# A two-layer mixed-attention MoE block on one core: small token blocks of an expert in one go, and the loop for left-over tokens in the midst of the experts

## Chip, cores, metric

One core of a Trainium2 chip runs the whole program; nothing is shared with other cores. The metric is the device time in microseconds, of the kernel before the median of three runs.

## What is computed

Two layers over 512 image tokens and, in the first layer, 256 context tokens, width 1024: three kinds of attention, a merge of their outputs, then a mixture of 16 experts of which each token takes two. The change touches the experts alone:

```python
def moe_ffn(tokens, w_router, b_router, w_gate, w_up, w_down):
    ...
    def expert_block(args):
        xb, e = args
        hid = jax.nn.silu(xb @ w_gate[e]) * (xb @ w_up[e])
        return hid @ w_down[e]

    y = lax.map(expert_block, (buf.reshape(n_blocks, MOE_BLOCK, d), block_e)).reshape(-1, d)
    contrib = y[dest] * sw[:, None].astype(y.dtype)
    return jnp.zeros_like(tokens).at[st].add(contrib)
```

`w_gate` and `w_up` are 1024 x 512 for each expert, `w_down` 512 x 1024, all float32. The result of a token is the weighted sum of its two experts.

## The kernel before

**Places for tokens.** The program is fixed ahead of the routing, so each of 16 places ("slots") takes one expert and a set number of tokens: `LINES` (line 1885) gives a letter for each. B is a `Block` of 128 tokens, S a `Half` of 64, P both together, 128+64, for the most wanted experts. Layer 0 has `BBBBPBSBBPBSBPBS`: three P, at slots 4, 9 and 13. Layer 1 has `BBBSBSSBSSBSSBSS`, no P. Slots 0 to 2 hold fixed experts; the router sorts the others by how many tokens they got. A token record lies in a table in DRAM; POOL fetches records (`lrec`), gathers their rows (`xg`) and, at an expert's end (`finish`, `add_up`, line 1567), adds the weighted output into DRAM (`yd` in layer 0, `xa` in layer 1).

**Left-over tokens.** Tokens that find no place are served by `late_block` (line 1705), a whole expert on 128 of them, in a loop whose trip count `nmore` the router works out (line 2095). The loop, `tc.For_i` in lines 1771 and 1772, stands ahead of all experts of a layer: behind the first gathers (`next_fetch`), ahead of SP's 13 reads of the expert order (line 1776) and of the first transposes. `LB` is the number of weight buffer sets in its body.

**Weights.** `Weights` (line 38) streams all weights in 512 KB chunks in a fixed list, four for each of gate (G), up (U) and down (D) of an expert. `load` issues the next chunk's DMA on SP whenever a raw buffer is free; in layer 0's experts there are 24 raw buffers, in layer 1's 31. `make` splits a chunk for a Block into two parts (`wh` on ScalarE, `wl` on VectorE, lines 102 and 114), after which its raw buffer goes back; there is room for the parts of four chunks. A Half reads the raw chunk itself. At a P slot the chunk is kept raw as well (`keep`) until `free`.

**TensorE.** A Block takes six matmuls a chunk, in three terms (`mm3`), stationary 128 columns, moving 512. A Half takes matmuls on two column halves of 64 (`up` in line 1654, `down` in 1679). Both are recorded under line 174, so the names tell them apart: `g<-wh,xH` or `yps<-wh,hidT` is a Block's, `g<-raw,xs` or `ysm<-raw,hidS` a Half's. For each slot the order is: transposes of the next slot's tokens (`turn`), up product of this slot, half of the next slot's gate product, transposes of this slot's hidden values (`hidden`), the other half, this slot's down product, `finish`. The helper that the change replaces takes the blocks of a slot chunk by chunk:

```python
ch = ws.get()
for i, b in enumerate(blocks[s]):
    b.up(ps[i], *words(b, ch), c)
used(ch)
```

Of the kernel before, what the change touches and what calls it, by code (L numbers as in the profile page):

```python
# [23 lines left out]
PG1 = 14  # L24
MW = 8
EX = {0: 3, 1: 5}
LB = 2
RING = 10


# [7 lines left out]
class Weights:  # L38
# [95 lines left out]
    def free_raw(self, c):  # L134
        self.live[id(c.raw_pool)] -= 1
        c.raw_pool = None
        self.load()

    def free(self, c):

        if c.part_pool is not None:
            self.live[id(c.part_pool)] -= 2
        if c.part_pool is None or c.keep:
            self.free_raw(c)
# [3 lines left out]
def tile_dit(ctx, tc, a, out):  # L148
    nc = tc.nc
# [8 lines left out]
    def acc_tile(name="acc"):  # L158
        return psum.tile([128, 512], F32, tag="acc", name=name)
# [21 lines left out]
    def split(h, l, src):  # L181
        nc.scalar.copy(h, src)
        nc.vector.tensor_tensor(l, src, h.bitcast(F32), op=OP.subtract)
# [59 lines left out]
    def w_of(l, what, e, c):  # L243

        w = a[{"G": "w_gate", "U": "w_up", "D": "w_down"}[what]][l]
        return w[e, c] if isinstance(e, int) else w[bass.ds(e, 1), c].rearrange("o p n -> (o p) n")
# [81 lines left out]
    ws = Weights(nc, specs)  # L328
# [144 lines left out]
    def mod_row(pool, tag, l, j, v, name):  # L473
        t = pool.tile([128, D], F32, tag=tag, name=name)
        nc.sync.dma_start(t, bc(modd[l][j, v, :], D))
        return t
# [1061 lines left out]
    def moe(l, R, late, ex):  # L1538
# [15 lines left out]
        def yo_tile():  # L1554
            return mx.tile([128, D], F32, tag="yo", name="yo", bufs=YO[l])

# [141 lines left out]
        def words(b, ch):  # L1698
            return (ch.raw,) if isinstance(b, Half) else (ch.h, ch.l)

        def used(ch):
            ws.pump(2, LEAD)
            ws.free(ch)

        def late_block(j):

            r = mx.tile([128, 4], I32, tag="rec2", name="rec2", bufs=1)
            at = mx.tile([128, 1], I32, tag="at2", name="at2", bufs=1)
            lst = mx.tile([128, 2, SLOTS], I32, tag="lst", name="lst", bufs=1)
            R.rest(lst, yo_tile())  # L1710
            nc.vector.tensor_copy(at, lst[:, 1, bass.ds(j, 1)])
            R.record(r, at)
            e = nc.values_load(lst[0:1, 0, bass.ds(j, 1)], engines=[mybir.EngineType.SP], min_val=0, max_val=NE - 1)
            w = [[mw.tile([128, 1024], dt, tag="mw", name=f"w2{i}{n}") for n, dt in enumerate((F32, F32R, F32R))]
                 for i in range(LB)]

            def part(what, i):
                raw, h, lo = w[i % LB]
                nc.sync.dma_start(raw, w_of(l, what, e, i % 4))
                split(h, lo, raw)  # L1720
                return h, lo

            b = Block(r)
            b.fetch(yo_tile())
            b.turn()
            g, u = acc_tile("g2"), acc_tile("u2")
            for i in range(8):
                b.up(g if i < 4 else u, *part("GU"[i // 4], i), i % 4)
            b.silu(g)
            b.times(u)  # L1730
            b.hidden()
            b.sums()
            for k in range(4):
                b.down(*part("D", 8 + k), k)
            b.finish()


        blocks, records = [], {}
        for s in range(NE):
# [4 lines left out]
            bs = [Half(lrec[:, s, :], slot=s) if kind == "S" else Block(lrec[:, s, :])]  # L1744
            records[bs[0]] = lrec[:, s, :], place(l, s)
            if kind == "P":
                i = PLACED[l].index(s)
# [6 lines left out]
        def next_fetch():  # L1754
            if queue:
                queue.pop(0).fetch()

        def next_record():
            if later:
                out_, i = records[later.pop(0)]  # L1760
                R.record(out_, R.pat[:, i:i + 1])

        def ahead():
            next_fetch()
            next_record()
# [2 lines left out]
        ws.low()  # L1768
        for _ in range(XG[l]):
            next_fetch()  # L1770
        with tc.For_i(0, nc.values_load(R.nmore[0:1, 0:1], min_val=0, max_val=SLOTS)) as j:
            late_block(j)
        ws.limit = first_in + NEAR if l == 0 else len(ws.specs)
        ws.load()
        for s in range(AHEAD, NE):
# [5 lines left out]
        ahead()  # L1781
        next_record()

        def gate(s, c0, c1, ps, done=None):

            for c in range(c0, c1):
                ch = ws.get()
                for i, b in enumerate(blocks[s]):
                    b.up(ps[i], *words(b, ch), c)
                    if c == 3 and done:  # L1790
                        done(i)
                used(ch)

        def products(s, name):
            return [b.product(name) for b in blocks[s]]

        def silus(s, ps):
            for b, p in zip(blocks[s], ps):
                b.silu(p)

        gp = products(0, "g")
        gate(0, 0, 4, gp)
        silus(0, gp)
        for s in range(NE):
            nx = s + 1 < NE
            if nx:
                for b in blocks[s + 1]:
                    b.turn()
                    ahead()
            up = products(s, "u")  # L1810
            gate(s, 0, 4, up, lambda i: blocks[s][i].times(up[i]))
            if nx:
                gp = products(s + 1, "g")
                gate(s + 1, 0, HIDAT, gp)
            for b in blocks[s]:
                b.hidden()
            if nx:
                gate(s + 1, HIDAT, 4, gp)
                silus(s + 1, gp)
            for b in blocks[s]:  # L1820
                b.sums()
            for k in range(4):
                ch = ws.get()
                for b in blocks[s]:
                    b.down(*words(b, ch), k)
                used(ch)
            if l == 0 and not nx:
                ws.pump(4 * len(TURN) + WEND)
            ws.low()
            for b in blocks[s]:  # L1830
                b.finish()
            if l == 0 and s == NE - 2:
                for j in range(2):
                    gt2.append(mod_row(pool0, "pg", 0, j, 5, f"gt2{j}"))
# [7 lines left out]
    for l in range(2):  # L1842
        ws.set_pools(2 * l, *mixer_pools)
        mixer(l)
        moe(l, *merge(l))
# [30 lines left out]
HT = {0: 2, 1: 1}  # L1876
TROWS = 896
MORE = 6
YO = {0: 2, 1: 1}
XG = {0: 2, 1: 1}  # L1880
NS = NE - AHEAD
SLOTS = 14
# [11 lines left out]
LEAD = 3  # L1894
# [23 lines left out]
class Router:  # L1918
# [3 lines left out]
    def __init__(self, tc, nc, rt, small, l, nt, tri, ones, br, oac_tile, tabd):  # L1922
# [10 lines left out]
        self.cap = small([128, NE], F32, "cap")  # L1933
        self.more = small([128, MORE, NE], F32, "more")
        self.spacer = small([1, 1], F32, "spacer")
        self.scat = []

    def prepare(self):
# [20 lines left out]
        nc.vector.memset(self.cap, 128.0)  # L1959
        nc.gpsimd.iota(self.more, pattern=[[128, MORE], [0, NE]], base=0, channel_multiplier=0,  # L1960
                       allow_small_or_imprecise_dtypes=True)
# [108 lines left out]
    def arrange(self, count):  # L2070
# [21 lines left out]
        tt(over, count, self.cap, op=OP.subtract)  # L2092
        tt(self.more, over[:, None, :].to_broadcast([128, MORE, NE]), self.more, op=OP.is_gt)
        nc.vector.reduce_sum(flag, self.more.rearrange("p b e -> p (b e)"), axis=AX.X)
# [142 lines left out]
```

## Time and profile before

| | |
|---|---|
| median of three runs | 2968.36 us (2964.67 to 2971.39) |
| profiled execution | 2971.79 us, span 2970.0 us |
| TensorE busy | 2774.9 us (93%), granted clock 0.969 in the mean |
| VectorE, ScalarE, GpSimd busy | 1835.0, 1279.9, 355.3 us |
| DMA | 557.63 MB, mean 188 GB/s |
| experts of layer 0, of layer 1 | about 1345 to 1663, and 2683 to 2946 us |

Times of the rows further down are microseconds from the start of the span. PE is TensorE, PEld its weight loads, DVE VectorE, ACT ScalarE, POOL GpSimd; SPq is SyncE's queue, which issues the weight DMAs. In brackets stands how long the engine was idle before an instruction and who released it. A busy share near 1 over the whole run says little by itself: the stages have different limits, so the stretches are read one by one.

### The profile page before, as it was taken

To read this page: it belongs to the slowest core of one execution; us is meant where nothing else is said; L and a number is where in the kernel's file an instruction comes from. 1 tells how busy PE (TensorE), PEld (TensorE's weight loads), DVE (VectorE), ACT (ScalarE), POOL (GpSimd) and SP (SyncE) were. 2 spreads that over 40 slices of the span, in tenths; PEclk is the share of its full clock that TensorE was granted. 3 is DMA by queue.
4 is the path that set the end of the run, shared out by engine and by line. 5 is a ranking of instruction groups with operands and counts; after the bars stand their busy time and mean duration, and the time that the engine had idled before them with its cause. 6 is when DMAs were issued, how large, how long until landed. Compare 5 with 4: busy or idle time off the path is not lost. (4 is left out here: it accounts for less than half of the span.)

```text
span 2970.0 us, 41952 instructions
## 1 busy us (share of the span) xinstructions
PE 2774.9 (93%) x15152; PEld 2221.7 (75%) x15152; DVE 1835.0 (62%) x3340; ACT 1279.9 (43%) x2370; POOL 355.3 (12%) x415
## 2 busy tenths in 40 slices
PE   7999999999999999979999699999999999978985
PEld 4888888888888766767666378878888887767653
DVE  4676567666554455677676566667776655677543
ACT  4444445445443211217575354444455442226332
POOL 1220000000010000022222131100000100012311
PEclk8999999999999999989999899999999999988998
DMA  6333222213243566758999732222223447589997
GB/s 240 131 110 105 89 75 91 91 65 103 100 156 118 211 240 238 273 225 304 328 370 363 256 122 82 89 78 97 75 96 123 146 153 285 207 304 341 370 367 293
DMA packets 201910, 557.63 MB, mean 188 GB/s; under 512 B 25158, under 2 KB 49862, under 8 KB 201696
## 3 DMA queue, kind: packets, MB, share of 16 engines
q1 hardware_dynamic: 173888, 503.63, 47.0%
q0 software_dynamic: 10688, 25.02, 3.5%
q10 hardware_dynamic: 17120, 26.23, 2.4%
q8 instruction: 121, 1.98, 0.3%
q14 instruction: 93, 0.76, 0.1%
HBM read 461.94 MB, written 96.77 MB: 188 GB/s over the span
## 5 line engine op out<-in xcount | busy, mean ns | idle before, releaser
L114 DVE TENSOR_TENSOR wl<-raw,wh 128x1024 fp32r<-128x1024 f32 x474 | 564.6, 1221 | 130.7 <-ACT wh L102 123.8
L102 ACT CAST wh<-raw 128x1024 fp32r<-128x1024 f32 x474 | 484.4, 1050 | 352.0 <-DMA raw<-oT 105.0
L887 ACT ACTIVATE P<-sc,st 128x768 f32<-128x768 f32 (+4 forms) x240 | 176.3, 734 | 339.9 <-DVE st L885 213.4
L885 DVE TENSOR_REDUCE st<-sc 128x1 f32<-128x768 f32 (+4 forms) x240 | 178.6, 744 | 121.5 <-PE sc L174 115.7
L174 PE MATMUL psb<-wl,wh 128*128 128x512 f32 x480 | 189.6, 395 | 8.1 <-DVE wl L114 8.0
L921 ACT CAST ptH<-pt 128x512 fp32r<-128x512 f32 x264 | 142.9, 591 | 125.0 <-PE pt L906 104.5
L174 PE MATMUL psb<-wh,wh 128*128 128x512 f32 x480 | 192.9, 402 | 1.7 <-ACT wh L102 1.7
L174 PE MATMUL psb<-wh,wl 128*128 128x512 f32 x480 | 189.1, 394 | 2.0 <-DVE wl L114 2.0
L931 DVE TENSOR_TENSOR ptL<-pt,ptH 128x512 fp32r<-128x512 f32 x264 | 169.6, 681 | 9.3 <-ACT ptH L921 9.1
L906 PE MATMUL pt<-ident,P 128*128 128x128 f32 x1056 | 141.5, 275 | 13.9 <-ACT P L887 10.9
L906 PEld LDWEIGHTS pt<-ident,P 128*128 128x128 f32 x1056 | 119.5, 141 | 45.2 <-ACT P L887 31.3
L174 PE MATMUL psR<-wh,hH 128*128 128x512 f32 (+1 forms) x384 | 150.8, 393 | 0.0
L174 PE MATMUL psR<-wl,hH 128*128 128x512 f32 (+1 forms) x384 | 147.1, 383 | 2.7 <-DVE wl L114 2.7
L174 PE MATMUL psR<-wh,hL 128*128 128x512 f32 (+1 forms) x384 | 147.6, 384 | 0.0
L893 DVE TENSOR_SCALAR P<-P,st 128x768 f32<-128x768 f32 (+3 forms) x240 | 130.0, 542 | 8.5
L174 PEld LDWEIGHTS psb<-wh,wh 128*128 128x128 f32 x480 | 91.1, 190 | 47.5 <-issue 19.3
L481 POOL TENSOR_SCALAR rstd<-ss 128x4 f32<-128x4 f32 (+2 forms) x70 | 22.0, 314 | 835.3 <-ACT h L487 303.1
L174 PEld LDWEIGHTS psb<-wl,wh 128*128 128x128 f32 x480 | 91.1, 190 | 29.1 <-DVE wl L114 11.5
L174 PE MATMUL sc<-swkT,swqs 128*128 128x256 f32 x704 | 109.1, 281 | 2.2 <-ACT P L887 2.2
L174 PEld LDWEIGHTS psb<-wh,wl 128*128 128x128 f32 x480 | 91.1, 190 | 22.9 <-DVE wl L114 3.6
L174 PE MATMUL yps<-wh,hidT 128*128 128x512 f32 x320 | 105.7, 397 | 0.0
L1094 DVE COPY sc<-sink 128x1 f32<-128x1 f32 x160 | 25.7, 161 | 128.5 <-PE sc L174 122.3
(495 smaller groups left out, 6916.4 us busy)
## 6 DMA issues: line engine op xcount, KB each, us to landing
raw<-in_w_in_dram SPq DMA_DIRECT2D x136, 512.0 KB
raw<-in_w_gate_dram SPq DMA_DIRECT2D x128, 512.0 KB
raw<-in_w_up_dram SPq DMA_DIRECT2D x128, 512.0 KB
raw<-in_w_down_dram SPq DMA_DIRECT2D x128, 512.0 KB
raw<-in_w_mod_dram SPq DMA_DIRECT2D x96, 512.0 KB
raw<-in_w_br_dram SPq DMA_DIRECT2D x48, 512.0 KB
raw<-oT SPq DMA_DIRECT2D x30, 512.0 KB
raw<-in_w_out_dram SPq DMA_DIRECT2D x16, 512.0 KB
```

The source lines that it names most:

```text
L102: self.nc.scalar.copy(c.h, c.raw)
L114: self.nc.vector.tensor_tensor(c.l, c.raw, c.h.bitcast(F32), op=OP.subtract)
L174: nc.tensor.matmul(ps, lhs, rhs, start=start, stop=stop, skip_group_check=share)
L481: nc.gpsimd.tensor_scalar(r[:, 0:cnt], ss, four / n, four * EPS, op0=OP.mult, op1=OP.add)
L885: nc.vector.reduce_max(st[:, 1, h:h + 1], s[:, 0:self.ns], axis=AX.X, negate=True)
L887: nc.scalar.activation(self.P[h][:, 0:self.ns], s[:, 0:self.ns], AF.Exp, bias=st[:, 1, h:h + 1], accum_out=st[:, 2, h:h + 1])
L893: nc.vector.tensor_scalar(self.P[h][:, 0:self.nk], self.P[h][:, 0:self.nk], st[:, 3, h:h + 1], None, op0=OP.mult)
L906: nc.tensor.transpose(pt[:, c * 256 + h * 128:c * 256 + (h + 1) * 128], self.P[2 * x + h][:, i * 128:(i + 1) * 128], ident)
L921: nc.scalar.copy(ph, src)
L931: nc.vector.tensor_tensor(pl, src, ph.bitcast(F32), op=OP.subtract)
L1094: nc.vector.tensor_copy(s[:, nk:nk + 1], sink[:, hd:hd + 1])
```

## The change

At a P slot, all four chunks of a product go through the Block first; each gives its parts back (`free_parts`) but stays raw in `kept`, and then the Half takes all four. This holds for gate, up and down (`chunk`). The loop for left-over tokens moves from ahead of the experts to behind slot 10 in layer 0 and slot 13 in layer 1 (`LOOPAT`), behind that slot's `finish`. Its body has one weight buffer set instead of two.

```diff
--- before.py
+++ after.py
@@ -24,7 +24,7 @@
 PG1 = 14
 MW = 8
 EX = {0: 3, 1: 5}
-LB = 2
+LB = 1
 RING = 10
 
 
@@ -135,6 +135,11 @@
         self.live[id(c.raw_pool)] -= 1
         c.raw_pool = None
         self.load()
+
+    def free_parts(self, c):
+
+        self.live[id(c.part_pool)] -= 2
+        c.part_pool = None
 
     def free(self, c):
 
@@ -1768,8 +1773,6 @@
         ws.low()
         for _ in range(XG[l]):
             next_fetch()
-        with tc.For_i(0, nc.values_load(R.nmore[0:1, 0:1], min_val=0, max_val=SLOTS)) as j:
-            late_block(j)
         ws.limit = first_in + NEAR if l == 0 else len(ws.specs)
         ws.load()
         for s in range(AHEAD, NE):
@@ -1781,15 +1784,33 @@
         ahead()
         next_record()
 
+        kept = []
+
+        def chunk(bs, c, step, done=None):
+
+
+            ch = ws.get()
+            step(0, c, words(bs[0], ch))
+            if c == 3 and done:
+                done(0)
+            if len(bs) == 1:
+                used(ch)
+                return
+            ws.pump(2, LEAD)
+            ws.free_parts(ch)
+            kept.append(ch)
+            if c == 3:
+                for i, ch in enumerate(kept):
+                    step(1, i, words(bs[1], ch))
+                    ws.free(ch)
+                kept.clear()
+                if done:
+                    done(1)
+
         def gate(s, c0, c1, ps, done=None):
 
             for c in range(c0, c1):
-                ch = ws.get()
-                for i, b in enumerate(blocks[s]):
-                    b.up(ps[i], *words(b, ch), c)
-                    if c == 3 and done:
-                        done(i)
-                used(ch)
+                chunk(blocks[s], c, lambda i, k, w: blocks[s][i].up(ps[i], *w, k), done)
 
         def products(s, name):
             return [b.product(name) for b in blocks[s]]
@@ -1820,15 +1841,15 @@
             for b in blocks[s]:
                 b.sums()
             for k in range(4):
-                ch = ws.get()
-                for b in blocks[s]:
-                    b.down(*words(b, ch), k)
-                used(ch)
+                chunk(blocks[s], k, lambda i, c, w: blocks[s][i].down(*w, c))
             if l == 0 and not nx:
                 ws.pump(4 * len(TURN) + WEND)
             ws.low()
             for b in blocks[s]:
                 b.finish()
+            if s == LOOPAT[l]:
+                with tc.For_i(0, nc.values_load(R.nmore[0:1, 0:1], min_val=0, max_val=SLOTS)) as j:
+                    late_block(j)
             if l == 0 and s == NE - 2:
                 for j in range(2):
                     gt2.append(mod_row(pool0, "pg", 0, j, 5, f"gt2{j}"))
@@ -1876,6 +1897,7 @@
 HT = {0: 2, 1: 1}
 TROWS = 896
 MORE = 6
+LOOPAT = {0: 10, 1: 13}
 YO = {0: 2, 1: 1}
 XG = {0: 2, 1: 1}
 NS = NE - AHEAD
```

TensorE in layer 0, slot 4, end of the first and start of the second chunk of the up product, before (`raw` are chunks as the Half reads them):

```order
L174 MATMUL u<-wl_13592,xH 128x512
L174 MATMUL u<-wh_13591,xL 128x512
L174 MATMUL u<-raw_13203,xs 64x256 x4
L174 MATMUL u<-wh_13601,xH 128x512
L174 MATMUL u<-wl_13602,xH 128x512
L174 MATMUL u<-wh_13601,xL 128x512
```

and of the change, the end of the same product:

```order
L179 MATMUL u<-wl_13431,xH 128x512
L179 MATMUL u<-wh_13430,xL 128x512
L179 MATMUL u<-raw_12989,xs 64x256 x4
L179 MATMUL u<-raw_13001,xs 64x256 x4
L179 MATMUL u<-raw_13013,xs 64x256 x4
L179 MATMUL u<-raw_13047,xs 64x256 x4
L179 MATMUL g<-wh_13440,xH 128x512
```

The Half's matmuls of four chunks stand together instead of one chunk's between two of the Block's.

SP at the end of layer 1, before: the last down weights of slot 15, then the final gain and the rows for the output.

```order
L83 DMA raw_27178<-in_w_down_dram 128x1024
L83 ISA
L83 DMA raw_27180<-in_w_down_dram 128x1024
L1852 DMA gf<-in_g_final_dram 128x1024
L1856 DMA cx_27423<-xa_116 128x1024
```

Of the change, with the semaphores that a row waits for (DMAHW are the eight that SP's DMAs raise):

```order
L83 DMA raw712_26961<-in_w_down_dram 128x1024 [waits DMAHW7_49,PE_49]
L83 ISA
L83 DMA raw713_26963<-in_w_down_dram 128x1024 [waits DMAHW0_49,DVE_49]
L1851 TENSOR_LOAD nmore_23306
L1851 ISA x2
L1851 COMPARE_AND_BRANCH
L1851 UNCONDITIONAL_BRANCH [waits SP_sequencer_49,DMAHW0_49,DMAHW1_49,DMAHW2_49,DMAHW3_49,DMAHW4_49,DMAHW5_49,DMAHW6_49,DMAHW7_49]
```

The loop of layer 1 now stands behind the same last down weights of slot 15 (`raw713` is the last chunk of the list), so behind the loads of all 20 chunks that slots 14 and 15 still use, and ahead of the final gain.

## Rows read from the trace of the kernel before

**Rows 1.** Stretches (us, busy by engine and count, PEclk, DMA share, GB/s): layers 0, 1, 1
```profile
1420.00:1445.00 25.00, 25.00 (x134) 17.07 (x134) 17.07 (x16) 15.52 (x18) 4.51 (x3) 1.00 0.92 313
...
2900.00:2925.00 25.00, 23.34 (x150) 15.72 (x148) 14.36 (x16) 9.43 (x12) 5.03 (x3) 1.00 1.03 385
...
2831.00:2834.00 3.00, 2.31 (x12) 1.79 (x14) 0.00 (x0) 0.49 (x1) 1.87 (x2) 0.66 0.98 386
```

**Rows 2.** Timeline (start, us, engine, line, instruction, idle before): start of layer 0's experts
```profile
1333.65 0.98 POOL L1549 DMA_INDIRECT xg<-h2d,rec  x1 [4.93 <-SPq L1771]
...
1341.79 1.97 PE L493 MATMUL xbt<-ident,xg 128*128 128x128 f32 x8 [17.05 <-SPq L1776]
...
1349.70 0.63 PE L174 MATMUL g<-wl,xH 128*128 128x512 f32 x1
```

**Rows 3.** Landings by line: layer 0's first gather, its middle adds, the last add
```profile
DMA to landing us min/median/max: 4.4/4.4/4.4
...
DMA to landing us min/median/max: 8.8/8.8/8.8
...
DMA to landing us min/median/max: 3.7/3.7/3.7
```

**Rows 4.** DMA issues of layer 1's experts: gathers, median us to landing
```profile
xg<-h2d,lrec POOLq DMA_INDIRECT x13, 10.0
```

**Rows 5.** Line of the loop, layer 1 (count, ns min/median/max, first and last start)
```profile
L1771 SPq COMPARE_BRANCH  x2: 33/38/44, 2672.8 to 2675.6; - x2
...
L1771 SPq EVENT_SEMAPHORE  x12: 27/28/28, 2678.4 to 2679.1; - x12
```

**Rows 6.** Timeline: start of layer 1's experts
```profile
2671.53 0.33 SPq L1563 DMA_DIRECT2D gt2row<-modd  x1
...
2680.06 1.97 PE L493 MATMUL xbt<-ident,xg 128*128 128x128 f32 x8 [14.04 <-issue]
...
2684.25 4.62 DVE L114 TENSOR_TENSOR wl<-raw,wh 128x1024 fp32r<-128x1024 f32 x4
...
2688.71 1.94 SPq L83 DMA_DIRECT2D raw<-in_w_gate_dram  x4
```

**Rows 7.** Timeline of TensorE: products of layer 0's fifth to seventh expert
```profile
1430.61 0.48 PE L174 MATMUL u<-wh,xH 128*128 128x512 f32 x1
...
1441.01 0.50 PE L174 MATMUL g<-wh,xH 128*128 128x512 f32 x1
...
1458.15 0.50 PE L174 MATMUL u<-wh,xH 128*128 128x512 f32 x1
...
1463.82 1.95 PE L174 MATMUL g<-raw,xs 128*64 128x256 f32 x16
...
1474.70 3.67 PE L174 MATMUL u<-raw,xs 128*64 128x256 f32 x32
...
1478.30 0.50 PE L174 MATMUL g<-wh,xH 128*128 128x512 f32 x1
```

**Rows 8.** Timeline: end of layer 0's eleventh expert
```profile
1572.70 0.39 PE L174 MATMUL yps<-wh,hidT 128*128 128x512 f32 x1
...
1574.57 1.61 POOL L1568 DMA_INDIRECT yd<-yo,lrec  x1 [3.01 <-ACT yo L1626]
```

**Rows 9.** Timeline: the last two experts of layer 1
```profile
2918.50 0.71 PE L1643 MATMUL xst<-ident,xg 64*128 64x64 f32 x8
...
2940.89 0.44 PE L1672 MATMUL hidt<-ident,gs 128*128 128x128 f32 x2 [0.59 <-DVE gs L1667]
...
2941.85 3.96 PE L174 MATMUL ysm<-raw,hidS 128*64 128x512 f32 x16 [0.52 <-ACT hidS L1674]
...
2944.72 0.20 PEld L174 LDWEIGHTS ysm<-raw,hidS 128*64 128x64 f32 x4 [0.96 <-DMA raw<-in_w_down_dram]
```

**Rows 10.** Timeline of TensorE in layer 1, after a wait for tokens
```profile
2831.70 1.77 PE L493 MATMUL xbt<-ident,xg 128*128 128x128 f32 x8 [2.42 <-DMA xg<-h2d,lrec]
...
2833.40 4.62 PE L174 MATMUL u<-raw,xs 128*64 128x256 f32 x32
```

## The prediction

> **What bounds the kernel now.** I read the page first, then the two expert stages in stretches, then the loop for left-over tokens at its present place, then the two places to which it goes. In layer 0 (experts from 1345 to 1660 us) TensorE is the bound: in the stretch with the first 128+64 expert it is busy for 25.00 of 25 us, while the DMA engines have a little left at a share of 0.92. In layer 1 it is the other way round: DMA share 1.03 at 385 GB/s, and TensorE has gaps, 23.34 of 25 us [rows 1]. So a microsecond of TensorE time counts in full in layer 0; in layer 1 TensorE runs just behind the weights, and what counts is when the last weights land and how much work is left then.
>
> The loop has no work here: its trip count is zero, and none of its weight loads appears in the trace. What it costs is its meeting of all engines. In layer 1 SP's last DMA ahead of it went out at 2671.53 [rows 6]; SP passed its own part of the meeting only at 2675.6, 4 us later, and then each engine went through 12 semaphore events that began at 2678.4 [rows 5]. That is when the gather of tokens was in: it takes 4.4 us to land [rows 3] and so went out at about 2674. I read this as: **nobody leaves the loop before every DMA issued ahead of it, weights included, has landed**. From 2678.4 to the first transposes at 2680.06 [rows 6] the meeting itself took 1.7 us.
>
> **The 128+64 experts.** There are three, all in layer 0, each with three products of four chunks. Before, a chunk is six full-width matmuls and then the small ones; now the small ones of all four chunks run in one go. The u product of the first took 1430.61 to 1441.01 = 10.40 us. The same full-width part by itself, in the next expert, took 1458.15 to 1463.82 = 5.67, and the small part by itself, in the one after, 1474.70 to 1478.30 = 3.60 [rows 7]. Together 9.27, so 1.13 a product goes into the to and fro. Nine products: 10.2 at most. I take 9.5, since the transposes of the hidden step stand between the second and third chunk of a g product in both orders and are a change of shape of their own. The lower bound is nothing, if the weights don't come faster (a rival below). Four raw chunks now stay until the small part instead of being given back one by one. I cost that at nothing: TensorE was busy through the whole stretch [rows 1], so weights were ahead; without that lead it would cost up to the whole gain.
>
> **The loop leaves the start of the experts.** Layer 0: the first block needs one gather, issued at 1333.65 [rows 2], in 4.4 us later [rows 3], at 1338.05; the transposes began only at 1341.79 [rows 2], since the loop also waited for a second gather and held its meeting. Gain 3.7 at most; I take 3.5. One weight load comes free ahead of that gather, too little to disturb it much; the bound on the other side is 0.
>
> Layer 1: without the meeting the start comes 1.7 us earlier at most. But SP now passes four weight loads at about 2674, as the gather starts. Gathers that run amid weights took 10.0 to land [rows 4], against 4.4 for this one [rows 3], so the start lies between 1.7 earlier and 4 later; I take no change. The Trainium skill, "DMA: Bandwidth & Descriptors", section "Issuing engines are not separate DMA queues", says that DMAs of different engines share the same 16 DMA engines and interleave; by that alone the gather lands late, and this start would be up to 4 us worse instead of unchanged. The trace agrees for gathers within the stage; whether four loads suffice, no row shows.
>
> What helps layer 1 is SP itself: its 13 reads of the expert order stood behind the loop and held it until 2688.71, though the first of four freed buffers was there at 2684.25 + 1.2 = 2685.5 [rows 6]. Now these reads fall into the wait for the gather. The weight stream, the bound there, comes 0 to 4 us earlier; I take 2.5.
>
> **The loop in layer 0, after the eleventh expert.** At that place TensorE ended the down product at 1572.70 + 0.4 = 1573.1, and POOL issued the expert's add into DRAM at 1574.57 [rows 8]. Before, TensorE goes straight on. Now it waits until that add and all weights on their way are in. An add amid weights takes 8.8 to land, a half-size one on quiet queues 3.7 [rows 3]; the queues drain meanwhile, so I take 6, near the middle, and give the weights issued just ahead the same time. Landing at 1580.6, meeting 1.7: TensorE stands for 9.2 us (6.9 to 12). Behind the loop wait, on SP, the next up weights, which costs nothing while the buffers are full; on ACT and VectorE the next casts, which nobody can use earlier; on POOL the next gather, an expert ahead of its use. Then the clock: after an idle of 2.4 us eight transposes took 1.77 and 32 small matmuls 4.62 [rows 10], at a granted clock of 0.66 over those 3 us [rows 1]. The small ones take 3.67 at full clock [rows 7], so about 1.0 was lost, and some 0.8 on the transposes, which took 1.97 at the half level [rows 2]. After a longer stop I take 2.5 (1.8 to 4; at the start of the stage a matmul still took 0.63 eight us after the first transposes [rows 2], half of 8 being the upper end). Sum 11.7 (8.7 to 16).
>
> **The loop in layer 1, after the fourteenth expert.** This is the large term. Two experts of 64 tokens remain, 20 weight chunks. The order of SP has all 20 ahead of the loop, because there are more buffers than that; behind it are only the final gain and the rows of the output. Before, TensorE is through with the fourteenth expert at 2918.50 and then eats the chunks as they land, until 2941.85 + 3.96 = 2945.8; its last wait for weights ended at 2944.72 [rows 9]. With the loop it stands from 2918 on until the last chunk is in, and only then begins: 2944.7, less 2.5 from the earlier stream, plus 1.7 for the meeting, is 2943.9. Work left: five products of 3.60 [rows 7] = 18.0; 0.7 of transposes of the last tokens; two hidden steps, 0.4 and, exposed, 0.59 + 0.44 + 0.52 = 1.5 [rows 9]: 20.6. Clock 2.5 as above. End 2967.0 against 2945.8: **+21.2** (19 to 25.2, by 4 to 0 us from the stream and 1.8 to 4 of clock). The tail behind it (last add, norm, output) stays as long.
>
> The smaller LB touches the loop's body alone, which isn't run: nothing.
>
> **Sum.** -3.5 - 9.5 + 11.7 + 21.2 = +19.9. The profiled execution took 2971.79, so 2991.7 in its terms; the three timed runs have a median 3.4 lower, 2968.36, so I forecast **2988**, with 2979 to 2998 for this case.
>
> **Rivals.**
> *Layer 0 becomes bound by DMA.* If the full-width parts, closer together now, or the raw chunks held longer starve TensorE, the 9.5 is not gained: 2998. For it: a share of 0.92, and 1.03 is what the bound stage shows, so there is no more than a tenth to spare. Against it: 9.5 of 315 us is 3%. Chance 0.12.
> *The loop in layer 1 costs half.* If the meeting lets part of the 20 chunks land later, some of the last two experts still overlaps the stream: some 10 us less, 2978. Against it: the order on SP. Chance 0.08.
> *The loop is nearly free in the midst.* If the meeting waits only for what its neighbours need, it costs 1.7 and 1.8 of clock in layer 0, 3.5, and in layer 1 hides behind the weights: -3.5 - 9.5 + 3.5 - 2.5 = -12, **2956, faster**. It decides at one point, whether SP's wait in layer 1 lasts until the last expert's weights are in. Against it: the 4 us in which SP stood for a transfer of the final scale that no engine needed yet [rows 5, 6]. Chance 0.05.
> That the change doesn't group the small matmuls can be left aside: the order shows them together.
>
> **Numbers.** Forecast 0.75, the rivals 0.12, 0.08 and 0.05. The range takes in the forecast's own, the first rival and the upper half of the second: 2978 to 3001. No change means within 0.2%, 5.9 us, about what a measurement can tell. Slower 0.93 (forecast, first two rivals, less a little), same 0.03, faster 0.04.
>
> **What the profile of the changed kernel will show.** Right: TensorE idle for some 25 us late in layer 1, ended by the loop, and then five products of small matmuls without a wait for DMA; an idle of 7 to 12 us in layer 0 after the eleventh expert; small matmuls of the 128+64 experts in runs of 32 over 3.6 us, and 1 us less for each product; the first transposes of layer 0 under 1 us behind the landing of the first gather. Wrong: waits of TensorE for weights inside layer 0's experts; weights still landing after the loop in layer 1; an idle at the loops of only 2 us.

## The result, and the profile after

| | before | after |
|---|---|---|
| median of four runs | 2967.76 us | 2996.27 us (2988.52 to 2997.76) |
| profiled execution, span | 2971.79, 2970.0 us | 2997.76, 2996.0 us |
| granted clock, mean | 0.969 | 0.966 |

The ratio is 1.009, with a 95% interval of 1.0069 to 1.0111: 28.5 us slower, forecast were 19.9. Where it went is read in five places.

The timeline of TensorE in the first 128+64 expert of layer 0 (start, us, instruction), beside [rows 7]:

```profile
1431.45 0.48 PE L179 MATMUL u<-wh,xH 128*128 128x512 f32 x1
...
1437.22 3.67 PE L179 MATMUL u<-raw,xs 128*64 128x256 f32 x32
...
1440.83 0.50 PE L179 MATMUL g<-wh,xH 128*128 128x512 f32 x1
```

The 32 small matmuls stand together, and the u product takes 9.38 us instead of 10.40. But its full part took 5.77 and not 5.67. That small excess is in every full matmul (128x128 against 128x512) of both expert stages. The u product of the second expert has 24 of them; here are its second and its last, of before and then of after:

```profile
1372.13 0.39 PE L174 MATMUL u<-wl,xH 128*128 128x512 f32 x1
...
1377.14 0.39 PE L174 MATMUL u<-wh,xL 128*128 128x512 f32 x1
```

```profile
1372.78 0.39 PE L179 MATMUL u<-wl,xH 128*128 128x512 f32 x1
...
1377.91 0.39 PE L179 MATMUL u<-wh,xL 128*128 128x512 f32 x1
```

22 steps: 5.01 / 22 = 0.2277 us before, 5.13 / 22 = 0.2332 after. The duration shown (0.39) is the same, and the granted clock of layer 0's experts is 1.00 in both ([rows 1], and the first row of the stretches below): the difference shows only in the starts.

The place of layer 0's loop, after the eleventh expert (beside [rows 8]):

```profile
1570.12 0.40 PE L179 MATMUL yps<-wh,hidT 128*128 128x512 f32 x1
...
1572.12 1.61 POOL L1573 DMA_INDIRECT yd<-yo,lrec  x1 [3.11 <-ACTq L1851]
...
1582.07 1.97 PE L498 MATMUL xbt<-ident,xg 128*128 128x128 f32 x8 [11.55 <-issue]
1583.97 4.78 PE L179 MATMUL u<-raw,xs 128*64 128x256 f32 x32
```

TensorE stands for 11.55 us, and then 32 small matmuls take 4.78 instead of 3.6.

The start of layer 1 (beside [rows 6]):

```profile
2671.67 0.15 DVE L2117 CAST nmore<-bw 128x1 int32<-128x1 f32 x1
...
2675.99 1.76 SPq L83 DMA_DIRECT2D raw<-in_w_up_dram  x4
2675.99 0.99 POOL L1554 DMA_INDIRECT xg<-h2d,rec  x1 [4.07 <-DVE wl L114]
...
2683.90 1.94 PE L498 MATMUL xbt<-ident,xg 128*128 128x128 f32 x8 [15.96 <-DMA raw<-in_w_up_dram]
```

The first row is the router's end, which serves as a landmark below. The gather leaves together with four weight loads, and the transposes come 12.23 us after the router's end; before it was 10.32 (2669.74 to 2680.06).

Layer 1's loop and what is left behind it (beside [rows 9]), then stretches of after (columns as in [rows 1]):

```profile
2948.47 1.11 PE L1648 MATMUL xst<-ident,xg 64*128 64x64 f32 x8 [26.05 <-SPq L1851]
2949.51 6.37 PE L179 MATMUL u<-raw,xs 128*64 128x256 f32 x32
...
2959.68 3.60 PE L179 MATMUL ysm<-raw,hidS 128*64 128x512 f32 x16
2963.11 3.62 PE L179 MATMUL u<-raw,xs 128*64 128x256 f32 x32
2967.33 0.44 PE L1677 MATMUL hidt<-ident,gs 128*128 128x128 f32 x2 [0.60 <-DVE gs L1672]
2968.29 3.65 PE L179 MATMUL ysm<-raw,hidS 128*64 128x512 f32 x16 [0.52 <-ACT hidS L1679]
```

```profile
1420.00:1445.00 25.00, 25.00 (x148) 18.49 (x147) 16.46 (x17) 14.85 (x18) 5.51 (x3) 1.00 0.91 291
1570.00:1582.00 12.00, 0.52 (x3) 0.09 (x1) 0.00 (x0) 1.11 (x1) 1.61 (x1) 0.61 0.72 251
1582.00:1595.00 13.00, 12.93 (x68) 9.06 (x70) 6.18 (x6) 5.36 (x7) 1.88 (x2) 0.84 0.89 299
2925.00:2947.00 22.00, 0.00 (x0) 0.00 (x0) 0.00 (x0) 0.00 (x0) 0.58 (x1) 0.50 0.82 308
2949.00:2960.00 11.00, 11.00 (x74) 6.47 (x74) 0.42 (x1) 1.06 (x3) 0.00 (x0) 0.73 0.15 49
```

For 26 us nothing computes while the last weights stream in; the clock is at its lower level, 0.50, and the first small product behind takes 6.37 us. Then all runs without a wait for weights.

Between landmarks, in the profiled executions (us; R is the router's end, T the first transposes, E the end of the last down product; `group_alone`, `pad192` and `held` are experiments below):

| | before | group_alone | after | pad192 | held |
|---|---|---|---|---|---|
| layer 0, R to T | 13.3 | 13.6 | 10.2 | 10.1 | 10.1 |
| layer 0, T to E | 321.4 | 310.8 | 330.2 | 324.4 | 322.5 |
| layer 1, R to T | 10.3 | 10.3 | 12.2 | 12.3 | 12.5 |
| layer 1, T to E | 265.8 | 266.2 | 288.0 | 287.5 | 271.8 |

The parts that the change does not touch differ by some us from one execution to the next (the mixer of layer 1 took 1006.5 us in the one of before, 999.4 in that of after), so causes are told from this table, and times from the medians.

### The profile page after: what moved, and what is told of

Read it like the earlier page. It is cut to its first block, busy times and chain, and to the rows that moved or that the text cites. A ratio compares the mean times of both kernels' runs of the same rounds, so it can differ in the third digit from the quotient of the medians.

```text
span 2996.0 us, 41959 instructions
## 1 busy us (share of the span) xinstructions
PE 2769.7 (92%) x15152; PEld 2225.4 (74%) x15152; DVE 1833.9 (61%) x3340; ACT 1277.6 (43%) x2368; POOL 357.6 (12%) x415
## 5 line engine op out<-in xcount | busy, mean ns | idle before, releaser
L911 PE MATMUL pt<-ident,P 128*128 128x128 f32 x1056 | 141.5, 275 | 13.9 <-ACT P L892 11.0
L179 PEld LDWEIGHTS psb<-wl,wh 128*128 128x128 f32 x480 | 90.7, 189 | 27.6 <-DVE wl L114 10.2
```

Source lines behind the costliest of these rows:

```text
L179: nc.tensor.matmul(ps, lhs, rhs, start=start, stop=stop, skip_group_check=share)
L911: nc.tensor.transpose(pt[:, c * 256 + h * 128:c * 256 + (h + 1) * 128], self.P[2 * x + h][:, i * 128:(i + 1) * 128], ident)
```

## Experiments

**The two parts apart.** The grouping with the loop at its old place, and the moved loop with the experts chunk by chunk:

```diff
+        with tc.For_i(0, nc.values_load(R.nmore[0:1, 0:1], min_val=0, max_val=SLOTS)) as j:
+            late_block(j)
         ws.limit = first_in + NEAR if l == 0 else len(ws.specs)
...
-            if s == LOOPAT[l]:
-                with tc.For_i(0, nc.values_load(R.nmore[0:1, 0:1], min_val=0, max_val=SLOTS)) as j:
-                    late_block(j)
```

That is `group_alone`, against the changed kernel; `loop_alone` is the kernel before with these lines the other way round, `LOOPAT` as in the change and LB 1.

> The 128+64 experts in one go, LB 1, the loop at its old place ahead of the experts. Prediction's step: -9.5 us against before (0 to -10.2), so about 2958. Rival, the gain is eaten by waits for weights or by a slower pace of the full matmuls: 0, 2968. In the changed kernel's profile the full 128x512 matmuls of both expert stages follow each other every 0.2334 us, before every 0.228; if grouping brings that, it shows here and costs about 7 us in layer 0.

> Before, with the loop moved behind slots 10 and 13 and LB 1, the 128+64 experts chunk by chunk as before. Prediction's steps: -3.5 + 11.7 + 21.2 = +29.4, about 2997. Rival, the slower pace of the full matmuls (0.2334 us a step in both expert stages of the changed kernel, 0.228 before) comes with the moved loop: then it shows here, and the time is 5 to 10 us above that sum, 3002 to 3007.

The grouping alone: 2955.35 us, ratio 0.9955 (0.9939 to 0.9972), 13.9 us less in the median; in the table layer 0's experts are 10.6 shorter. The u product of the first 128+64 expert takes 9.25 us:

```profile
1431.96 0.48 PE L179 MATMUL u<-wh,xH 128*128 128x512 f32 x1
...
1437.61 3.67 PE L179 MATMUL u<-raw,xs 128*64 128x256 f32 x32
...
1441.21 0.50 PE L179 MATMUL g<-wh,xH 128*128 128x512 f32 x1
```

The step of the full matmuls is 0.2277. The loop alone: 3006.26 us, ratio 1.0127 (1.0108 to 1.0147), 37 us more, with a step of 0.2332. So the moved loop brings the slower pace, and costs more than its two stops.

**LB, and the change once more.** The edit of `lb_alone`, against the kernel before; `after_again` has none:

```diff
-LB = 2
+LB = 1
```

> Before, with LB 1 alone. Prediction's step: nothing, within 0.2% of before, and a step of 0.228 us from one full matmul to the next in the expert stages. Rival, the place of the buffers makes the slower pace: 0.2334 us there, and 7 to 10 us more.

> The changed kernel once more. If the slower pace of the full matmuls in both expert stages (0.2334 us a step) belongs to the change, it is there again and the median is again 2996. If it belongs to one execution, the step is 0.228 us, and the profiled execution comes in at about 2988, as one of the four runs did.

LB alone: 0.9998 (0.9988 to 1.0007), nothing. The changed kernel again: 2996.52 us and again 0.233 in both stages. The pace belongs to the program.

**Why the pace changes.** A tile gets its memory when it is first asked for. With the loop ahead of the experts, its small tiles (record, row, list: 192 bytes) and the output rows `yo` (8192) are asked for before the transposed tokens `xH`, `xL` and the hidden values `hidT`; with the loop in the midst, after them. By the addresses in the built programs, layer 0's `xH` starts at byte 198272 before and at 189888 after the change; the weight parts `wh` and `wl` stay at 148608 and multiples of 4096 from there. What counts below is the rest by 256, that is, what is left of a start address after division by 256: the 8192 bytes leave it as it is, the 192 change it.

`pad192` is the changed kernel with one unused tile of 48 words, `pad64` with one of 16; `off64` is `group_alone` with 16 words ahead of its loop:

```diff
         for _ in range(XG[l]):
             next_fetch()
+        mx.tile([128, 48], I32, tag="pad", name="pad", bufs=1)
         ws.limit = first_in + NEAR if l == 0 else len(ws.specs)
```

> The changed kernel with 64 unused bytes put ahead of the transposed tokens. Theory: before, the loop's small tiles (list, record) took their memory ahead of the transposed tokens and hidden values, which so began at multiples of 128 bytes; with the loop moved they come later and these tiles begin 64 bytes off (189888 = 1483.5 x 128 instead of 198272 = 1549 x 128), and a full matmul takes a step of 0.2334 us for 0.228. The pad puts them at multiples of 128 again: step 0.228, the experts of layer 0 about 5 us shorter (936 matmuls x 0.0054), so 2990 to 2992; layer 1 hardly changes. Rival, the pace comes from the loop standing in the midst: 0.2334 stays, and 2996.

> The changed kernel with 192 unused bytes in place of the 64, so that the transposed tokens and hidden values leave the same rest by 256 bytes (128) as the weight parts, as they do before the change; with the pad of 64 the rest was 0, in the changed kernel 192. Theory: the pace of the full matmuls hangs on moving and stationary operand having the same rest by 256: step 0.228 us in both expert stages, experts of layer 0 some 5 us shorter than the changed kernel's 329.6 (first transposes to last down product), about 2990. Rival, the loop's place itself makes the pace: 0.233, and 2996.

> The small blocks in one go with both loops at the start (2955), with 64 unused bytes ahead of the transposed tokens, so that their rest by 256 bytes is 192, as in the changed kernel. By the theory of the rest: step 0.2334 us, experts of layer 0 about 5 us longer than 310.8, about 2960. Rival, the loop's place makes the pace: 0.228 and 2955.

| | rest of `xH` by 256 bytes (`wh`: 128) | step, us, second expert of layer 0 | median, us |
|---|---|---|---|
| before | 128 | 0.2277 | 2967.28 to 2969.27 |
| group_alone | 128 | 0.2277 | 2955.35 |
| off64 | 192 | 0.2332 | 2961.81 |
| after | 192 | 0.2332 | 2996.27, 2996.52 |
| pad64 | 0 | 0.2332 | 2997.46 |
| pad192 | 128 | 0.2277 | 2993.14 |

The first guess, a start at multiples of 128 bytes, fell with `pad64`. The second holds in both directions: 192 unused bytes bring the fast pace back with the loop in its new place, and 64 take it away with the loop in its old one. The same two matmuls in `pad192`:

```profile
1367.80 0.39 PE L179 MATMUL u<-wl,xH 128*128 128x512 f32 x1
...
1372.81 0.39 PE L179 MATMUL u<-wh,xL 128*128 128x512 f32 x1
```

and in `off64`:

```profile
1371.77 0.39 PE L179 MATMUL u<-wl,xH 128*128 128x512 f32 x1
...
1376.90 0.39 PE L179 MATMUL u<-wh,xL 128*128 128x512 f32 x1
```

5.01 / 22 = 0.2277, and 5.13 / 22 = 0.2332. The fast pace is worth 5.8 us of layer 0's experts (330.2 to 324.4) and 5.7 in the other direction (310.8 to 316.5); in layer 1, which waits for weights, next to nothing. The median moved by 3 us with `pad192`, which is not clear of noise (ratio 1.0081, 1.0063 to 1.0099, against 1.009 of the changed kernel), and by 6.5 with `off64`. The Trainium skill, "SBUF — State Buffer", section "Operand start alignment", asks that an operand start at a multiple of its element's size, and says that this is about legality, not speed. All these do; what it leaves open, the speed, does differ here. Whether the two operands must have the same rest, or each a rest of 128, these runs do not tell apart; a rest of 64 was not tried.

**What the loop in layer 1 costs.** One expert later (`slot14`, against `pad64`), and behind the last one (`end_layer1`, with 15 there, the 64 bytes in layer 1 alone, and layer 0's loop at its old place):

```diff
-LOOPAT = {0: 10, 1: 13}
+LOOPAT = {0: 10, 1: 14}
```

> The same with layer 1's loop one expert later, behind the fifteenth. If nobody leaves the loop before all weights are in, what it costs in layer 1 is the work that is left then: two products of 3.60 us (one expert's up and down), about 1.5 of hidden step, 1.7 meeting and 2.5 clock, 12 to 14 us instead of about 21.5 behind the fourteenth; so 9 us less than with the pad alone, 2981 to 2983. Rival, the cost is a fixed price of a stop in the midst: no change from the pad alone.

> Small token blocks in one go, layer 0's loop at its old place at the start, layer 1's behind the last expert. No work is left behind the loop there and the last add must land anyway, so it costs 2 to 5 us at the end (meeting, and what SP issues behind it), against 1.7 saved at layer 1's start less 2 to 3 of a later gather beside the weights: 2955 to 2961, about the same as the grouping alone (2955).

Behind the fifteenth expert: 2985.10 us, 12.4 less than `pad64`, where 9 were expected; from R to E of layer 1 the profile gives 289.7 us instead of 299.5, 9.8 less. TensorE then stands 9.99 us at the loop:

```profile
2943.34 6.62 PE L179 MATMUL u<-raw,xs 128*64 128x256 f32 x32 [9.99 <-SPq L1852]
```

No fixed price, then: it falls with the work that is left. Behind the last expert: 2961.65, ratio 0.9978 (0.9969 to 0.9987), a shade above its range and 6 above `group_alone`. The profile has 2.3 of a later start, 1.8 regained within the stage and 4.0 more at the end, from the last product to the end of the span. It also has both paces in one program: 0.228 in layer 0, where the rest is 128, and 0.233 in layer 1, where it is 0.

**Fewer loads ahead of the loop.** The direct test of "nobody leaves the loop before every DMA issued ahead of it has landed", against `pad192`:

```diff
-        ws.limit = first_in + NEAR if l == 0 else len(ws.specs)
+        ws.limit = first_in + NEAR if l == 0 else len(ws.specs) - 12
...
+            if l == 0 and s == LOOPAT[l]:
+                ws.limit = ws.loaded
             for b in blocks[s]:
                 b.hidden()
...
                     late_block(j)
+                ws.limit = first_in + NEAR if l == 0 else len(ws.specs)
+                ws.load()
```

> The changed kernel with the 192 bytes, and weight loads held back until behind the loop: in layer 0 the 5 loads that go out during the last half of the eleventh expert, in layer 1 the last 12 chunks of 20. If nobody leaves the loop before all that was issued is in, TensorE's idle in layer 1 falls from 26 us to about 10 (12 x 1.36 less) and the last chunk lands about 5 us later than before the change, so layer 1 ends 16 to 20 us earlier than with the pad alone; in layer 0 the idle falls from 11.5 to about 8 if the weights end it, and stays if the add does. Sum 2968 to 2975. Rival, the stop has a price of its own: both idles stay, and the 12 chunks come on top, 2990 or more.

2975.23 us, 18 less than `pad192`, ratio to before 1.0024 (1.0012 to 1.0035); just above the expected range. Layer 1 in the timeline, with SP's loads:

```profile
2923.90 1.94 SPq L83 DMA_DIRECT2D raw<-in_w_down_dram  x4
2926.03 2.29 SPq L83 DMA_DIRECT2D raw<-in_w_up_dram  x4
2928.51 4.20 SPq L83 DMA_DIRECT2D raw<-in_w_down_dram  x4
```

```profile
2924.36 1.11 PE L1648 MATMUL xst<-ident,xg 64*128 64x64 f32 x8 [10.69 <-issue]
2925.40 5.83 PE L179 MATMUL u<-raw,xs 128*64 128x256 f32 x32
...
2943.63 3.65 PE L179 MATMUL ysm<-raw,hidS 128*64 128x512 f32 x16 [0.52 <-ACT hidS L1679]
```

With 12 of 20 chunks behind the loop the same work, through the same loop at the same place, stands 10.69 us instead of 25.81 in `pad192` (26.05 in the changed kernel), and the stage is 15.7 us shorter (287.5 to 271.8). In layer 0, with five loads less, the idle fell from 11.9 (in `pad192`) to 9.1. The add issued just ahead of that loop took 9.0 us to land in `pad192` and 6.3 in `held`, which is as much less:

```profile
DMA to landing us min/median/max: 9.0/9.0/9.0
```

```profile
DMA to landing us min/median/max: 6.3/6.3/6.3
```

**The start of layer 1.** With the loop at the start, SP's reads ahead of it (`start_reads`, against `group_alone`):

```diff
-        for _ in range(XG[l]):
-            next_fetch()
+        for s in range(AHEAD, NE):
+            slot_e[l, s] = nc.values_load(R.order[0:1, place(l, s):place(l, s) + 1],
+                                          engines=[mybir.EngineType.SP], min_val=0, max_val=NE - 1)
+        next_fetch()
         with tc.For_i(0, nc.values_load(R.nmore[0:1, 0:1], min_val=0, max_val=SLOTS)) as j:
             late_block(j)
+        for _ in range(XG[l] - 1):
+            next_fetch()
...
-        for s in range(AHEAD, NE):
-            slot_e[l, s] = nc.values_load(R.order[0:1, place(l, s):place(l, s) + 1],
-                                          engines=[mybir.EngineType.SP], min_val=0, max_val=NE - 1)
```

With the loop in the midst, the four loads behind the reads (`gather_first`, against `pad192`):

```diff
-        ws.load()
+        if l == 0:
+            ws.load()
         for s in range(AHEAD, NE):
```

> Small token blocks in one go, both loops at the start, but SP's 13 reads of the expert order stand ahead of the first gather and the loop, and in layer 0 one gather instead of two ahead of the loop. The prediction's step: layer 1's weight stream 2.5 us earlier (0 to 4), and about 2 us from layer 0's start: 2950 to 2955. Rival, the stream in layer 1 follows the buffers that come free, not SP's reads: then layer 1 takes as long as with the grouping alone (266 us from the first transposes to the last down product, its landing 275 us behind the router's end).

> The changed kernel with the 192 bytes, and at layer 1's start the four free weight loads behind SP's 13 reads of the expert order instead of ahead of them, so that the first gather of tokens runs on quiet queues. If the four loads delay that gather, the first transposes start 8.5 to 10 us behind the router's end instead of 12.25 (with the meeting, before the change, 10.3). Rival, the gather isn't held up by them and the wait is for something else: 12 us again. In the time at the end it should not show, since the loop behind the fourteenth expert waits for the weights, which come up to 4 us later: 2991 to 2997.

`start_reads`: 2958.36 us, ratio 0.9966 (0.9953 to 0.9979), not told apart from `group_alone`. Layer 0 starts 2 us earlier (R to T 11.6 instead of 13.6), but in layer 1 R to E is 276.1 us against 276.4: no gain in the time. That does not say that the reads hold nothing up. The first loads of layer 1 that need a freed buffer are these, in `group_alone`, `start_reads`, the changed kernel and `gather_first`, in this order:

```profile
2676.00 1.94 SPq L83 DMA_DIRECT2D raw<-in_w_gate_dram  x4
...
2672.81 3.74 SPq L83 DMA_DIRECT2D raw<-in_w_gate_dram  x4
...
2689.43 3.74 SPq L83 DMA_DIRECT2D raw<-in_w_gate_dram  x4
...
2680.47 3.74 SPq L83 DMA_DIRECT2D raw<-in_w_gate_dram  x4
```

| | before | group_alone | start_reads | after | gather_first |
|---|---|---|---|---|---|
| R to T | 10.3 | 10.3 | 12.0 | 12.2 | 9.7 |
| T to these loads | 8.7 | 8.5 | 5.4 | 5.5 | 5.5 |
| R to these loads | 19.0 | 18.8 | 17.5 | 17.8 | 15.2 |

Where the reads stand behind the loop, they hold these loads up by 3 us. Out of the way, the loads go out 5.4 to 5.5 us behind the first transposes; the casts that free the buffers stand behind those. In `start_reads` the transposes come 1.8 us later than in `group_alone`, so little of the gain is left.

`gather_first` in the timeline:

```profile
2669.58 0.99 POOL L1554 DMA_INDIRECT xg<-h2d,rec  x1 [4.08 <-DVE wl L114]
2674.92 1.57 PEld L498 LDWEIGHTS xbt<-ident,xg 128*128 128x128 f32 x8 [13.50 <-issue]
2674.95 1.94 PE L498 MATMUL xbt<-ident,xg 128*128 128x128 f32 x8 [13.44 <-DMA xg<-h2d,rec]
2675.03 1.75 SPq L83 DMA_DIRECT2D raw<-in_w_up_dram  x4
```

R to T is 9.7 us instead of 12.3. The landing of that first gather, in the changed kernel and then in this one:

```profile
DMA to landing us min/median/max: 7.1/7.1/7.1
```

```profile
DMA to landing us min/median/max: 4.5/4.5/4.5
```

I had not expected it in the time, and it came out at 2988.11, 5 us below `pad192`. In the profile R to E is 2.8 us shorter (296.9 and 299.7). Half of that is the last weights: TensorE goes on behind the loop 275.0 us after the router's end instead of 276.4. The other half is the clock, which came back sooner in this execution. The first product behind the loop, in `pad192` (granted clock 0.70 in the mean of the 11 us from there) and then in `gather_first` (0.83):

```profile
2947.66 6.26 PE L179 MATMUL u<-raw,xs 128*64 128x256 f32 x32
...
2941.28 4.85 PE L179 MATMUL u<-raw,xs 128*64 128x256 f32 x32
```

The other 2 us of the medians are not explained.

The lowest median of all is that of `group_alone`: 2955.35 us, below both kernels.

## Why the prediction came out as it did

- **The small blocks in one go, -9.5:** right. 10.6 in the table, and 9.25 for the u product where the sum of its parts was 9.27. The rival of a layer 0 bound by DMA is out: no wait for weights on TensorE there, with the grouping alone or with the whole change.
- **Layer 0's start, -3.5:** right, 13.3 to 10.2 is -3.1.
- **The loop in layer 0, +11.7:** a little small. With the pace set right it is 324.4 - 310.8 = 13.6. The step that was mis-sized is the landing, "I take 6": 6.3 is what the add takes with the weights held back; with them on the way it took 9.0 in `pad192`, about the upper end (8.8 for an add amid weights). In the changed kernel TensorE stood 11.55 us, for 9.2. The clock was sized right: 4.78 - 3.6 and 1.97 - 1.03, some 2.1 for 2.5.
- **The loop in layer 1, +21.2:** 24.2 in the table. The mechanism is shown by `held` and `slot14`. The work behind it took 2948.47 to 2971.94 = 23.5 us, forecast 20.6 + 2.5. But it began 276.8 us behind the router's end, where 2943.9 meant 274.2. The step that failed is "The weight stream, the bound there, comes 0 to 4 us earlier; I take 2.5": with the 1.7 of the meeting taken off, the last weights were in 275.1 us behind the router's end, and before 275.0 (2944.72 in [rows 9]). SP's reads did hold the stream up, as was read: now it starts 5.5 us behind the first transposes instead of 8.7. But its buffers come free behind those transposes, and they came 1.9 later; so it started only 1.2 earlier, and at its end nothing of that was left. Even 2.5 us at the transposes made 1.4 at the last weights (`gather_first`); where the rest goes, no run shows.
- **Layer 1's start, no change:** it came 1.9 us later, within its bounds of -1.7 and 4 (and is part of the 276.8). Four loads are enough to disturb the gather, 7.1 us to land instead of 4.4 [rows 3] or 4.5. The missing meeting gives back only 0.9 of that: from landing to transposes it is 0.8 us instead of 1.7. No change was the wrong choice between the bounds. The rule of the Trainium skill that the prediction cites there, of DMA engines that interleave, pointed the right way.
- **What no step had:** the pace of the full matmuls, 5.8 us in layer 0. The change was costed by the instructions that move. That a moved piece of code also moves the memory of its neighbours was not looked at; it is the largest part of what the sum lacked. By the table: -3.1 - 10.6 + 13.6 + 5.8, and 24.2 for layer 1 (R to E, 276.1 to 300.3), is 29.9; forecast were 19.9, and the medians differ by 28.5.
- **The range:** that 2996 lies inside it is in part luck. Its upper end, 2998, was the price of a layer 0 bound by DMA, which did not come; a pace that no step had came near it in its place.
- **The rivals:** half the cost, or nearly none, in the midst: both out by 26.05 and 11.55 us of idle. The point named for the last, whether SP waits for the last expert's weights, was the right one to look at.

## What to carry to other kernels

A loop that all engines enter together waited here for the transfers issued ahead of it, even with no trip: put such a loop where queues are empty and little work is left, or hold loads back until behind it. Costing a move, look also at which tiles get other addresses. Such a pace is found by dividing the distance of two starts by the steps between them, since neither durations nor granted clock show it.

## What was unexpected of the hardware

Full 128x512 matmuls follow each other at one of two paces at a granted clock of 1.00, by the addresses alone: 0.227 to 0.229 in the expert stages where the stationary operand's start leaves a rest of 128 by 256 bytes, like the weight parts', 0.232 to 0.234 at a rest of 192 or 0. All 13 kernels that were run fall on the side that their rest gives, in both layers. What in the memory makes the difference, no run here shows.
